# Two fused transformer blocks on one core: the last feature tile moved to the end of first products, and one-hot work moved from GpSimd to VectorE

## The chip, the core and the metric

The program runs on one core of a Trainium2 chip. A core has a matrix engine (TensorE, in rows PE; its weight loads are PEld), VectorE (DVE), ScalarE (ACT), GpSimd (POOL) and SyncE (SP, which here only issues DMAs). The engines work side by side; each takes its own instructions strictly in order and waits on semaphores for the others. The metric is the device time of one execution in microseconds (us).

## What is computed

A sequence of 512 tokens of width 1024 goes through two blocks. The first has a mixer (latent attention beside retention) and then a layer of 16384 small experts, of which each token uses 128: eight heads pick 16 experts each by two top-16 searches over 128 keys. The second block has pooling and sparse attention, and a feed-forward layer. The part that the change touches most is the expert layer:

```python
v1, i1 = lax.top_k(s1, PEER_TOPK)
v2, i2 = lax.top_k(s2, PEER_TOPK)
cand = (v1[..., :, None] + v2[..., None, :]).reshape(T, PEER_HEADS, PEER_TOPK * PEER_TOPK)
sc, ci = lax.top_k(cand, PEER_TOPK)
e1 = jnp.take_along_axis(i1, ci // PEER_TOPK, axis=-1)
e2 = jnp.take_along_axis(i2, ci % PEER_TOPK, axis=-1)
eidx = (e1 * PEER_NKEYS + e2).reshape(T, PEER_HEADS * PEER_TOPK)
gates = jax.nn.softmax(sc, axis=-1)
...
act = jax.nn.gelu(jnp.einsum('td,tkd->tk', xt, peer_u[it]), approximate=False)
return jnp.einsum('tk,tkd->td', gt * act, peer_v[it])
```

## The kernel before

Products in float32 accuracy are made from two rounded parts of each operand, a high and a low one (`wh` and `wl` for weights, and likewise for activations). `fm` (line 245) makes one product of 128 output features as three passes over the 8 tiles of the inner dimension: high by high, high weights by low activations, low weights by high activations, 24 matmuls in all. `split` (lines 210 and 211) makes the parts: ScalarE rounds the high part, and VectorE or GpSimd subtracts it for the low part (`wl`).

`residual` (line 367) is the product that ends a layer and is added to the stream: eight products over the activation tiles that the step ahead of it has just made. It is called six times: after the mixer of block one (activations `mgh`/`mgl`), after that of block two (`m2h`/`m2l`), and once for each of the four quarters of the feed-forward layer (`fh`/`fl`). In its first product, k = 0, the last of the eight tiles is the one made last.

In the expert layer, three token tiles (t = 0, 1, 2) are multiplied with all experts in turn, and the fourth (t = 3) gathers the rows of its experts. The stage between the queries and the big loop over experts does four things at once:

- `topkeys` and `topk` (VectorE): the searches, and then for each tile the picks, lines 1043 to 1055: a one-hot `oh` of 128x1024 by comparison (VectorE, line 1048), its product with the key numbers (GpSimd, line 1052, in four pieces of 128x256), and a sum over the one-hot (VectorE, line 1054). There are four such picks per tile and 16 in all.
- `spread` (line 1069): for 16 tokens at a time, four steps of one one-hot tile (`oh12` in the code, `oh` in rows) on VectorE (line 1077), four scalings of 128x128 with the gates (ScalarE, line 1083; for the third tile, t = 2, two of the four on GpSimd, line 1080), four small matmuls (line 1086, eight records in the trace for the four) and a copy to `stg` (ScalarE, line 1087); after four steps a DMA stores `stg` to `gates` in DRAM. A tile has 32 steps and the three tiles have 96.
- `front` (line 937): for one of the first 64 expert groups, a 512 KB load of `u_T`, its split (`wh` on ScalarE, `wl` on GpSimd), a product of 24 matmuls into `pu`, and a Gelu on ScalarE. Fronts 31 to 63 store their activations to DRAM (`ahead`).
- `step` (line 1106) decides in which program order these are interleaved: a front is added whenever `len(done_u) * PACE < steps + LEAD`. There are some 220 steps (19 of `topk` and 16 of `topkeys` per tile, 32 of `spread`), so that with `PACE` 3.6 the 64 fronts are all issued by the last step.

Outside the big loop the framework's scheduler then orders each engine's instructions; SyncE's DMAs stand in one queue as well. After the stage, the loop (`gated_acts`, `products`, rows `py`) loads `v` rows (`vr`) and the stored gates (`gin`), multiplies the activations with the gates on VectorE (line 1148), rounds them on ScalarE (`ah`) and multiplies.

Of the kernel before, what the change touches and what calls it, by code (L numbers as in the profile page):

```python
# [14 lines left out]
OP = mybir.AluOpType  # L15
AX = mybir.AxisListType

P = 128
T = 512
# [4 lines left out]
KD = D // P  # L24
# [142 lines left out]
def build(tc, A, OUT):  # L167
    nc = tc.nc
    es = ExitStack()
    V, S, G, TE = nc.vector, nc.scalar, nc.gpsimd, nc.tensor  # L170
# [71 lines left out]
        TE.matmul(out, lh, rl, start=False, stop=False)  # L242
        TE.matmul(out, ll, rh, start=False, stop=last)

    def fm(out, w, act, c0, t0, n, kt=KD, hooks=()):

        for i, (a, b) in enumerate(((0, 0), (0, 1), (1, 0))):
            for k in range(kt):
                TE.matmul(out, w[a][k][:, c0:c0 + P], act[b][k][:, t0:t0 + n],  # L249
                          start=i == 0 and k == 0, stop=i == 2 and k == kt - 1)  # L250
            if i < len(hooks):
                hooks[i]()

    def tm(out, w, act, c0, n, t0, m, kt=KD):

# [111 lines left out]
    def residual(get, act, sqs=None, norm=None):  # L367


        def done(k):  # L370
            def f(ps, a, b):
                V.tensor_tensor(h1[k][:, a:b], ps[:, a:b], h1[k][:, a:b], op=OP.add)  # L372
                if sqs:
                    sqs.add(h1[k], V if k > KD - 3 else G, a, b, k == KD - 1)
            return f
        for k in range(KD - 2 if sqs else KD):
            w, c0 = get(k)
            ps = mmps()
            fm(ps, w, act, c0, 0, T)
            done(k)(ps, 0, T)  # L380
        if sqs:
            js = [(mmps(), *get(k), done(k)) for k in (KD - 2, KD - 1)]
            for i, (a, b) in enumerate(HALVES):
                for j, (ps, w, c0, f) in enumerate(js):
                    fm(ps[:, a:b], w, act, c0, a, b - a, hooks=(lambda: norm.row(0),) if i and j else ())
                    f(ps, a, b)
                    if i and not j:
                        norm.cols(0)
# [116 lines left out]
    c = ks(half_slot("ckv", F32R))  # L505
# [7 lines left out]
    for a, b in PIECES:  # L513
        ps = mmps()
# [6 lines left out]
    for t0, t1, m in ((0, NT, P), (NT, NT + 1, M)):  # L521
        h = t1 - t0
# [86 lines left out]
    for h in range(8):  # L609
        b = 64 - h % 2 * 64  # L610
# [122 lines left out]
    for h in range(8):  # L733
# [11 lines left out]
        b = h % 2 * 64  # L745
# [65 lines left out]
    for h in range(8):  # L811
        w = wfm("w_rg", h)
        ps = mmps()
# [183 lines left out]
    def topk(t):  # L997

        val, idx = tops[t]


        cand = tn.tile([P, 8, 80], F32, name="cand", bufs=1)
        for o, a, na, nb_ in ((0, 0, 1, 16), (16, 1, 7, 8), (72, 8, 8, 1)):
            dst = cand[:, :, o:o + na * nb_].rearrange("p h (a b) -> p h a b", a=na)
            V.tensor_tensor(dst, val[:, 0, :, a:a + na, None].to_broadcast([P, 8, na, nb_]),
                            val[:, 1, :, None, :nb_].to_broadcast([P, 8, na, nb_]), op=OP.add)
        yield
        sel = tn.tile([P, 8, 16], F32, name="sel", bufs=1)
        pos = tn.tile([P, 8, 16], U32, name="pos", bufs=1)
        for h in range(8):  # L1010
            sc_ = tn.tile([P, P], F32, name="tscr", tag="tscr", bufs=2)
            top16(sel[:, h], pos[:, h], cand[:, h], sc_[:, :80])
            yield

        gate = tn.tile([P, 8, 16], F32, name="gate", bufs=1)
        V.tensor_tensor(gate, sel, sel[:, :, 0:1].to_broadcast([P, 8, 16]), op=OP.subtract)
        S.activation(gate, gate, AF.Exp)
        gs = tn.tile([P, 8], F32, name="gs", bufs=1)
        V.tensor_reduce(gs, gate, axis=AX.X, op=OP.add)
        V.reciprocal(gs, gs)  # L1020
        V.tensor_tensor(gate, gate, gs[:, :, None].to_broadcast([P, 8, 16]), op=OP.mult)
        yield

        pu = pos.rearrange("p h j -> p (h j)")
        row = tn.tile([P, 128], U32, name="prow", tag="tscr", bufs=2)
        col = tn.tile([P, 128], U32, name="pcol", tag="tscr", bufs=2)
        V.tensor_single_scalar(row, pu, 3, op=OP.logical_shift_right)
        V.tensor_single_scalar(col, pu, 7, op=OP.bitwise_and)
        af = tn.tile([P, 128], F32, name="af", bufs=1)
        bf = tn.tile([P, 128], F32, name="bf", bufs=1)  # L1030
        x = tn.tile([P, 128], F32, name="rk1", bufs=1)
        V.scalar_tensor_tensor(x, row, 9.0, col, op0=OP.is_equal, op1=OP.mult)
        V.tensor_scalar(af, row, 1.0, 0.0, op0=OP.subtract, op1=OP.max)
        V.tensor_tensor(af, af, x, op=OP.add)
        V.tensor_scalar(bf, row, 1.0, 8.0, op0=OP.is_equal, op1=OP.mult)
        V.tensor_tensor(x, col, x, op=OP.subtract)
        V.tensor_tensor(bf, bf, x, op=OP.add)
        yield

        idf = tn.tile([P, 2, 128], F32, name="idf", bufs=1)  # L1040
        V.tensor_copy(idf, idx.rearrange("p b h j -> p b (h j)"))
        ef = tn.tile([P, 2, 128], F32, name="ef", bufs=1)
        for b, rk_ in ((0, af), (1, bf)):
            iv = idf[:, b].rearrange("p (h r) -> p h r", h=8)
            for c in range(2):
                r_ = rk_[:, 64 * c:64 * c + 64, None]
                oh = tn.tile([P, 64, 16], F32, name="oh", bufs=2)
                V.tensor_tensor(oh, iota[:, None, :16].to_broadcast([P, 64, 16]), r_.to_broadcast([P, 64, 16]),
                                op=OP.is_equal)
                ov = oh.rearrange("p (h j) r -> p h j r", h=4)  # L1050
                for h in range(4):
                    G.tensor_tensor(ov[:, h], ov[:, h], iv[:, 4 * c + h, None].to_broadcast([P, 16, 16]), op=OP.mult)  # L1052
                yield
                V.tensor_reduce(ef[:, b, 64 * c:64 * c + 64], oh, axis=AX.X, op=OP.add)
                yield
        if t == GT:
            V.scalar_tensor_tensor(ef[:, 0], ef[:, 0], float(P), ef[:, 1], op0=OP.mult, op1=OP.add)
            V.tensor_copy(eg, ef[:, 0])
            V.tensor_copy(gg, gate.rearrange("p h j -> p (h j)"))
            return  # L1060
        pt = tpps()
        TE.transpose(pt[:, 0:P], ef[:, 0], ident)
        TE.transpose(pt[:, P:2 * P], ef[:, 1], ident)
        TE.transpose(pt[:, 2 * P:3 * P], gate.rearrange("p h j -> p (h j)"), ident)
        eT = tn.tile([P, 3, P], F32, name="eT", bufs=2)
        V.tensor_copy(eT, pt[:, :3 * P].rearrange("p (a t) -> p a t", a=3))
        picks[t] = eT

    def spread(t):
        NPL = (0, 0, 2)[t]  # L1070

        t0, eT = t * P, picks[t]
        for b0 in range(0, P, TB):
            stg = tn.tile([P, P, TB], F32, name="stg", bufs=2)
            for q0 in range(0, TB, 4):
                a1 = tn.tile([P, 2, 4, P], F32, name="oh12", bufs=4)
                V.tensor_tensor(a1, iota[:, None, None, :].to_broadcast([P, 2, 4, P]),  # L1077
                                eT[:, :2, b0 + q0:b0 + q0 + 4, None].to_broadcast([P, 2, 4, P]), op=OP.is_equal)
                for q in range(NPL):
                    G.tensor_tensor(a1[:, 1, q], a1[:, 1, q], eT[:, 2, b0 + q0 + q:b0 + q0 + q + 1].to_broadcast([P, P]),  # L1080
                                    op=OP.mult)
                for q in range(NPL, 4):
                    S.activation(a1[:, 1, q], a1[:, 1, q], AF.Copy, scale=eT[:, 2, b0 + q0 + q:b0 + q0 + q + 1])
                ps = mmps()
                for q in range(4):
                    TE.matmul(ps[:, q * P:(q + 1) * P], a1[:, 1, q], a1[:, 0, q], start=True, stop=True)  # L1086
                S.copy(stg[:, :, q0:q0 + 4], ps.rearrange("p (q e) -> p e q", q=4))
                yield
            nc.sync.dma_start(gd[:, :, (t0 + b0) // TB].rearrange("g p x -> p g x"),
                              stg.rearrange("p (g e) t -> p g (e t)", e=NE))  # L1090
# [8 lines left out]
        for x in g:  # L1099
            yield from x  # L1100

    PACE, LEAD = 3.6, 10
    steps = [0]

    def step():
# [60 lines left out]
    with tc.manual_schedule(engines={mybir.EngineType.Pool, mybir.EngineType.DVE}):  # L1166
        parts, u = gated_acts(0), u_of(AHEAD)
        for e in range(P - 2):
# [10 lines left out]
            while len(todo) > max(0, min(ngather, (P - 3 - e) * ngather // (P - 2 - G0))):  # L1179
                src, f, k = todo.pop(0)  # L1180
# [96 lines left out]
    kt = pool("keytmp", stack=stk)  # L1277
# [22 lines left out]
    for x in range(2):  # L1300
# [8 lines left out]
        for hf in range(2):  # L1309
            w = sp_.tile([P, 8, 256], F32, name="wc1", tag="h")  # L1310
            nc.sync.dma_start(w.rearrange("p l c -> p (l c)"), A["w_c1"][x][:, hf * 2048:(hf + 1) * 2048])
            w1.append(w)
    for br in range(2):
        w = wfm("w_kv", 2 * br)
        ps = mmps()
# [3 lines left out]
        for g in range(2):  # L1319
            a, b = slice(g * 64, g * 64 + 64), slice(64 - g * 64, 128 - g * 64)  # L1320
# [4 lines left out]
        w = wfm("w_kv", 2 * br + 1)  # L1325
        ps = mmps()
# [10 lines left out]
    w = wfm("w_gn", 0, width=48)  # L1337
    ps = mmps()
# [11 lines left out]
    ps = bank("s", "hid")  # L1350
# [149 lines left out]
    for g in range(4):  # L1500
        w = wfm("w_u", g)
        ps = mmps()
# [21 lines left out]
    for g, d in enumerate(pooled):  # L1524
        ps = bank("s", "yp")
# [43 lines left out]
    for b in range(4):  # L1569
        f = tuple(ks(slot(n, F32R)) for n in ("fh", "fl"))  # L1570
        for c in range(4):
# [4 lines left out]
            else:  # L1576
                for j in range(2):
                    ps = mmps()
# [47 lines left out]
```

## Time and profile before

| | |
|---|---|
| median of 3 runs | 2754.16 us (2748.56 to 2754.52) |
| the profiled execution | 2753.92 us |
| its span, first to last instruction | 2752.1 us |
| TensorE busy / its weight loads | 95% / 81% of the span |
| VectorE, ScalarE, GpSimd busy | 61%, 42%, 37% |
| mean granted TensorE clock | 0.977 of full speed |

The time of the profiled execution holds 1.8 us beside its span. The busy share of TensorE says little by itself, since its matmuls overlap and their ends are modelled; where it stood still is read from the chain of waits and from the idle times.

### The profile page before, as it was taken

The page shows a single profiled execution, that of the slowest core. Times are in us where ns is not written, and L with a number is a line of the kernel's source. Part 1 is how long each engine was busy: PE and PEld are TensorE (multiplying, and loading weights), DVE is VectorE, ACT ScalarE, POOL GpSimd, SP SyncE. Part 2 cuts the span into 40 slices and gives each one's busy share as a digit, 9 for nine tenths or more (in the row PEclk, how much of TensorE's full clock was granted, in tenths as well). Part 3 has the DMA queues.
Part 4 walks back from the last instruction along what each step waited for, and adds up shares of the span by engine and source line. Part 5 has one row for each costly group of instructions (what it writes and reads, how often), then busy time and mean ns, then how long its engine had stood idle before and what let it go on. Part 6 is the DMA issues. An engine that isn't in the chain of part 4 may idle for free.

```text
span 2752.1 us, 37185 instructions
## 1 busy us (share of the span) xinstructions
PE 2611.7 (95%) x13809; PEld 2239.1 (81%) x13809; DVE 1685.1 (61%) x3302; ACT 1149.3 (42%) x2096; POOL 1018.1 (37%) x735
## 2 busy tenths in 40 slices
PE   7899999999898998999999999998999999999998
PEld 6668778798898887888888888887666787878886
DVE  5672442248797863788888888886678422533433
ACT  4462332243676553333333333333677422423322
POOL 3322132326546690355555554552222233211111
PEclk9999999999999999999999999998999999999999
DMA  3312123323355567799999998983211123222221
GB/s 110 106 58 82 65 73 126 113 83 101 113 168 174 173 188 269 254 364 387 362 361 334 337 335 321 332 313 116 58 32 36 50 93 98 108 92 92 92 97 57
DMA packets 175653, 462.65 MB, mean 168 GB/s; under 512 B 15600, under 2 KB 76656, under 8 KB 168816
## 3 DMA queue, kind: packets, MB, share of 16 engines
q1 hardware_dynamic: 135152, 321.30, 33.4%
q0 software_dynamic: 36864, 134.23, 13.9%
q10 hardware_dynamic: 3456, 4.76, 0.7%
q8 instruction: 108, 1.77, 0.3%
q14 instruction: 73, 0.60, 0.1%
HBM read 419.59 MB, written 35.85 MB: 165 GB/s over the span
## 4 chain that ended last, share of the span: by engine, by line
PE 68%; DVE 10%; POOL 6%; issue 5%; DMA 4%; ACT 3%; ACTq 0%; SPq 0%; DVEq 0%; POOLq 0%
PE mm L249 34%; PE pu L249 12%; PE py L1158 11%; PE mm L1086 2%; POOL oh L1052 2%; POOL row L957 2%; PE o L1484 1%; PE tp L1479 1%; DVE row L962 1%; POOL wl L211 1%; DMA act<-ahead 1%; DVE vl L211 1%; DMA t<-t 1%; DVE oh L1077 1%; POOL oh L1080 1%
## 5 line engine op out<-in xcount | busy, mean ns | idle before, releaser
L211 POOL TENSOR_TENSOR wl<-wr,wh 128x1024 fp32r<-128x1024 f32 (+3 forms) x135 | 324.2, 2402 | 551.0 <-ACT wh L210 241.6
L210 ACT CAST wh<-wr 128x1024 fp32r<-128x1024 f32 (+2 forms) x271 | 274.3, 1012 | 411.4 <-PE mm L249 209.0
L249 PE MATMUL pu<-xf,wh 128*128 128x384 f32 x2048 | 392.4, 344 | 6.8 <-ACT act L944 6.8
L249 PEld LDWEIGHTS pu<-xf,wh 128*128 128x128 f32 x2048 | 362.9, 191 | 13.1 <-ACT act L944 7.9
L957 POOL DMA_INDIRECT row<-in_u_rows_dram,eg x128 | 187.2, 1463 | 245.5 <-DVE row L962 218.8
L957 POOL DMA_INDIRECT row<-in_v_rows_dram,eg x128 | 194.8, 1522 | 187.2 <-DVE yg L972 160.3
L211 DVE TENSOR_TENSOR wl<-wr,wh 128x1024 fp32r<-128x1024 f32 (+2 forms) x136 | 161.0, 1184 | 103.8 <-PE mm L249 63.6
L249 PE MATMUL pu<-xf,wl 128*128 128x384 f32 x1024 | 206.9, 345 | 14.7 <-POOL wl L211 14.0
L1158 PE MATMUL py<-vh,ah 128*128 128x512 f32 x768 | 198.8, 394 | 21.1 <-ACT ah L210 20.2
L249 PEld LDWEIGHTS pu<-xf,wl 128*128 128x128 f32 x1024 | 185.8, 193 | 18.2 <-POOL wl L211 17.0
L1158 PE MATMUL py<-vl,ah 128*128 128x512 f32 x768 | 198.0, 392 | 1.0 <-DVE vl L211 1.0
L1158 PE MATMUL py<-vh,al 128*128 128x512 f32 x768 | 196.0, 390 | 0.0
L210 ACT CAST vh<-vr 128x1024 fp32r<-128x1024 f32 x128 | 134.6, 1052 | 139.5 <-PE py L1158 74.2
L211 DVE TENSOR_TENSOR vl<-vr,vh 128x1024 fp32r<-128x1024 f32 x128 | 156.2, 1220 | 57.0 <-ACT vh L210 56.9
L1158 PEld LDWEIGHTS py<-vh,ah 128*128 128x128 f32 x768 | 143.3, 189 | 50.5 <-ACT ah L210 24.5
L1077 DVE TENSOR_TENSOR oh<-iota,eT 128x1024 f32<-128x1024 f32 x96 | 159.3, 1687 | 40.0 <-PE mm L1086 23.6
L210 ACT CAST ah<-act 128x384 fp32r<-128x384 f32 x128 | 65.6, 513 | 266.9 <-DVE act L1148 258.7
L1158 PEld LDWEIGHTS py<-vl,ah 128*128 128x128 f32 x768 | 145.5, 190 | 32.0 <-DVE vl L211 1.4
L1158 PEld LDWEIGHTS py<-vh,al 128*128 128x128 f32 x768 | 144.6, 188 | 30.1
L972 DVE SCALAR_TENSOR_TENSOR yg<-row,ag,yg 128x1024 f32<-128x1024 f32 x127 | 164.9, 1298 | 5.2 <-DMA row<-in_v_rows_dram,eg 2.9
L962 DVE SCALAR_TENSOR_TENSOR row<-row,xg 128x1024 f32<-128x1024 f32 x128 | 151.4, 1219 | 7.3 <-DMA row<-in_u_rows_dram,eg 7.2
L372 DVE TENSOR_TENSOR h<-mm,h 128x512 f32<-128x512 f32 (+1 forms) x54 | 34.1, 632 | 184.7 <-PE mm L249 184.7
(458 smaller groups left out, 5172.2 us busy)
## 6 DMA issues: line engine op xcount, KB each, us to landing
wr<-in_u_T_dram SPq DMA_DIRECT2D x128, 512.0 KB, 4.6
vr<-in_v_rows_dram SPq DMA_DIRECT2D x128, 512.0 KB, 6.3
wwr<-in_w_f_dram SPq DMA_DIRECT2D x32, 1024.0 KB, 4.8
gates<-stg SPq DMA_DIRECT2D x24, 1024.0 KB, 7.1
gin<-gates SPq DMA_DIRECT2D x16, 1536.0 KB, 10.6
wr<-in_w_gm_dram SPq DMA_DIRECT2D x16, 512.0 KB, 3.4
ahead<-act SPq DMA_DIRECT2D x33, 192.0 KB, 2.9
act<-ahead SPq DMA_DIRECT2D x33, 192.0 KB, 7.7
```

What stands on the lines that cost most here:

```text
L210: S.copy(hi, src)
L211: (lo_eng or V).tensor_tensor(lo, src, hi.bitcast(F32), op=OP.subtract)
L249: TE.matmul(out, w[a][k][:, c0:c0 + P], act[b][k][:, t0:t0 + n], start=i == 0 and k == 0, stop=i == 2 and k == kt - 1)
L372: V.tensor_tensor(h1[k][:, a:b], ps[:, a:b], h1[k][:, a:b], op=OP.add)
L957: G.indirect_dma_start(out=r, out_offset=None, in_=src, in_offset=bass.IndirectOffsetOnAxis(ap=eg[:, k:k + 1], axis=0))
L962: V.scalar_tensor_tensor(r, r, 1.0, xg, op0=OP.mult, op1=OP.mult, accum_out=ag[:, k:k + 1])
L972: V.scalar_tensor_tensor(yg[0], r, ag[:, k:k + 1], yg[0], op0=OP.mult, op1=OP.add)
L1052: G.tensor_tensor(ov[:, h], ov[:, h], iv[:, 4 * c + h, None].to_broadcast([P, 16, 16]), op=OP.mult)
L1077: V.tensor_tensor(a1, iota[:, None, None, :].to_broadcast([P, 2, 4, P]), eT[:, :2, b0 + q0:b0 + q0 + 4, None].to_broadcast([P, 2, 4, P]), ...
L1080: G.tensor_tensor(a1[:, 1, q], a1[:, 1, q], eT[:, 2, b0 + q0 + q:b0 + q0 + q + 1].to_broadcast([P, P]), op=OP.mult)
L1086: TE.matmul(ps[:, q * P:(q + 1) * P], a1[:, 1, q], a1[:, 0, q], start=True, stop=True)
L1158: TE.matmul(py[2 * t + d], x[:, t * P:(t + 1) * P], w[:, d * 512:(d + 1) * 512], start=e == 0 and i == 0, stop=e == P - 1 and i == 2)
```

## The change

The product of one-hot and key numbers in the picks goes from four GpSimd instructions to one on VectorE. The two scalings per step that GpSimd did for the third tile go to VectorE as `tensor_scalar`. `PACE` rises from 3.6 to 4.0, so that some 58 of the 64 fronts are issued by the last step and six follow it. And the first product of each `residual` handles the last activation tile after all passes over the other seven, with the pass over low weights ahead of that over low activations.

```diff
-    def fm(out, w, act, c0, t0, n, kt=KD, hooks=()):
-
-        for i, (a, b) in enumerate(((0, 0), (0, 1), (1, 0))):
-            for k in range(kt):
-                TE.matmul(out, w[a][k][:, c0:c0 + P], act[b][k][:, t0:t0 + n],
-                          start=i == 0 and k == 0, stop=i == 2 and k == kt - 1)
-            if i < len(hooks):
-                hooks[i]()
+    def fm(out, w, act, c0, t0, n, kt=KD, hooks=(), late=0):
+
+
+        for tiles in (range(kt - late), range(kt - late, kt)):
+            for i, (a, b) in enumerate(((0, 0), (1, 0), (0, 1)) if late else ((0, 0), (0, 1), (1, 0))):
+                for k in tiles:
+                    TE.matmul(out, w[a][k][:, c0:c0 + P], act[b][k][:, t0:t0 + n],
+                              start=i == 0 and k == 0, stop=i == 2 and k == kt - 1)
+                if i < len(hooks) and not late:
+                    hooks[i]()
+            if not late:
+                break
...
-            fm(ps, w, act, c0, 0, T)
+            fm(ps, w, act, c0, 0, T, late=1 if k == 0 else 0)
...
-                for h in range(4):
-                    G.tensor_tensor(ov[:, h], ov[:, h], iv[:, 4 * c + h, None].to_broadcast([P, 16, 16]), op=OP.mult)
+                V.tensor_tensor(ov, ov, iv[:, 4 * c:4 * c + 4, None].to_broadcast([P, 4, 16, 16]), op=OP.mult)
...
-                for q in range(NPL):
-                    G.tensor_tensor(a1[:, 1, q], a1[:, 1, q], eT[:, 2, b0 + q0 + q:b0 + q0 + q + 1].to_broadcast([P, P]),
-                                    op=OP.mult)
-                for q in range(NPL, 4):
+                for q in range(NV):
+                    V.tensor_scalar(a1[:, 1, q], a1[:, 1, q], eT[:, 2, b0 + q0 + q:b0 + q0 + q + 1], None, op0=OP.mult)
+                for q in range(NV, 4):
...
-    PACE, LEAD = 3.6, 10
+    PACE, LEAD = 4.0, 10
```

GpSimd's queue from the start of the stage, before, where `wl` is a front's low weights and `oh<-oh,idf` are the pieces of a pick:

```order
L211 TENSOR_TENSOR wl<-wr,wh 128x1024 x13
L1052 TENSOR_TENSOR oh<-oh,idf 128x256 x8
L211 TENSOR_TENSOR wl<-wr,wh 128x1024
L1052 TENSOR_TENSOR oh<-oh,idf 128x256 x8
L211 TENSOR_TENSOR wl<-wr,wh 128x1024 x7
L1052 TENSOR_TENSOR oh<-oh,idf 128x256 x3
```

and of the change, up to the first row gathers of the loop:

```order
L211 TENSOR_TENSOR wl<-wr,wh 128x1024 x64
L961 DMA row<-in_u_rows_dram,eg 128x1024 x2
L211 TENSOR_TENSOR wl<-wr,wh 128x1024
L961 DMA row<-in_u_rows_dram,eg 128x1024 x2
L211 TENSOR_TENSOR wl<-wr,wh 128x1024
```

Nothing stands between the low weights any more, and the first gathers move ahead of the last three of them. The end of the stage on TensorE, before (`mm<-oh` are the last steps of `spread`, `pu` fronts, `py` the loop's first product):

```order
L1086 MATMUL mm<-oh_9609 128x128 x4
L1086 MATMUL mm<-oh_9621 128x128 x4
L1086 MATMUL mm<-oh_9633 128x128 x4
L249 MATMUL pu<-xf,wh 128x384 x32
L1158 MATMUL py_9658<-vh,ah 128x512
```

and of the change:

```order
L1088 MATMUL mm<-oh_9381 128x128 x4
L251 MATMUL pu<-xf,wh 128x384 x16
L251 MATMUL pu<-xf,wl 128x384 x8
...
L251 MATMUL pu<-xf,wh 128x384 x16
L251 MATMUL pu<-xf,wl 128x384 x8
L1160 MATMUL py_9610<-vh,ah 128x512
```

Before, two thirds of two more fronts (16 of their 24 matmuls each, of the loop's own) stood between the last step and the loop; now six whole fronts stand there, and the loop's own follow later. SyncE's queue at the same place, of the change (`gates` is the last store of the stage, `gin` the first load of the loop):

```order
L1091 DMA gates<-stg 128x16x128
L950 DMA ahead<-act 128x384
L222 DMA wr<-in_u_T_dram 128x1024
L222 DMA vr<-in_v_rows_dram 128x1024
L1147 DMA gin<-gates 128x3072
L950 DMA ahead<-act 128x384 x2
```

The load of the gates stands ahead of the stores of the last five fronts, where it stood behind the last of all before. The first product of the first feed-forward quarter on TensorE, before (`fh`, `fl` are the activations, `wwh`, `wwl` the weights):

```order
L249 MATMUL mm<-fh,wwh 128x512 x10
L249 MATMUL mm<-fl,wwh 128x512 x8
L249 MATMUL mm<-fh,wwl 128x512 x8
L249 MATMUL mm<-fh,wwh 128x512 x6
```

and of the change:

```order
L251 MATMUL mm<-fh,wwh 128x512 x7
L251 MATMUL mm<-fh,wwl 128x512 x7
L251 MATMUL mm<-fl,wwh 128x512 x7
L251 MATMUL mm<-fh,wwh 128x512
L251 MATMUL mm<-fh,wwl 128x512
L251 MATMUL mm<-fl,wwh 128x512
```

Before, the scheduler had already put two matmuls of the second product in front; now 21 matmuls of the first product stand ahead of the one that needs the last tile.

## Rows read from the trace of the kernel before

**Rows 1.** The page, part 1: busy us, share of the span, instructions.

```profile
PE 2611.7 (95%) x13809; PEld 2239.1 (81%) x13809; DVE 1685.1 (61%) x3302; ACT 1149.3 (42%) x2096; POOL 1018.1 (37%) x735
```

**Rows 2.** Busy time by stretch of the stage: us, busy (instructions), granted clock, DMA.

```profile
618.80:690.50 71.70, 64.35 (x345) 62.84 (x343) 58.33 (x275) 23.90 (x30) 45.60 (x30) 0.95 0.30 100
690.50:815.00 124.50, 118.31 (x735) 116.09 (x736) 103.27 (x295) 86.74 (x212) 64.37 (x34) 0.96 0.47 142
815.00:938.00 123.00, 115.99 (x727) 113.96 (x726) 98.53 (x280) 83.61 (x196) 67.04 (x39) 0.97 0.58 175
938.00:1039.70 101.70, 90.20 (x566) 87.14 (x565) 64.98 (x52) 55.56 (x121) 87.96 (x89) 0.95 0.59 176
```

**Rows 3.** Groups by form in the stage, 618.8 to 1039.7 us.

```profile
L211 POOL TENSOR_TENSOR wl<-wr,wh 128x1024 fp32r<-128x1024 f32 x63 | 161.8, 2569 | 122.8 <-ACT wh L210 80.3 <-PE pu L249 35.5 <-ACT oh L1083 3.5
L1052 POOL TENSOR_TENSOR oh<-oh,idf 128x256 f32<-128x256 f32 x64 | 60.3, 974 | 22.2 <-DVE oh L1048 22.2
L1080 POOL TENSOR_TENSOR oh<-oh,eT 128x128 f32<-128x128 f32 x64 | 45.0, 733 | 5.7 <-DVE oh L1077 5.7
...
L1077 DVE TENSOR_TENSOR oh<-iota,eT 128x1024 f32<-128x1024 f32 x96 | 159.3, 1687 | 40.0 <-PE mm L1086 23.6 <-ACT stg L1087 5.0 <-POOL oh L1080 4.7
L1054 DVE TENSOR_REDUCE ef<-oh 128x64 f32<-128x1024 f32 x16 | 19.5, 1219 | 32.8 <-POOL oh L1052 32.7
...
L249 PE MATMUL pu<-xf,wl 128*128 128x384 f32 x512 | 106.7, 352 | 14.0 <-POOL wl L211 14.0
L1086 PE MATMUL mm<-oh 128*128 128x128 f32 x768 | 102.0, 282 | 11.2 <-POOL oh L1080 6.0 <-ACT oh L1083 5.0
L988 PE MATMUL mm<-keyst,pq 128*128 128x256 f32 x37 | 10.0, 391 | 0.0
```

**Rows 4.** Timeline of VectorE and GpSimd in the first picks: start, duration, instruction.

```profile
650.11 2.40 POOL L211 TENSOR_TENSOR wl<-wr,wh 128x1024 fp32r<-128x1024 f32 x1 [2.68 <-PE pu L249]
650.22 2.44 DVE L1016 TENSOR_TENSOR gate<-sel 128x128 f32<-128x128 f32 x1
...
657.24 0.28 DVE L1021 TENSOR_TENSOR gate<-gate,gs 128x128 f32<-128x128 f32 x1
657.91 1.22 DVE L1048 TENSOR_TENSOR oh<-iota,af 128x1024 f32<-128x1024 f32 x1
```

**Rows 5.** A VectorE scaling of 128x128 elsewhere in the kernel, by form.

```profile
L1467 DVE TENSOR_SCALAR s<-s,sm 128x128 f32<-128x128 f32 x24 | 5.6, 295 | 0.1
```

**Rows 6.** The chain of waits through the end of the stage: start, duration, what.

```profile
991.73 0.89 PE mm L1086 x8
992.62 4.20 PE pu L249 x24
...
1039.70 7.02 DMA gates<-stg
1046.79 9.19 DMA gin<-gates
1057.24 10.10 PE py L1158 x36
...
1068.74 8.20 PE py L1158 x36
```

**Rows 7.** Timeline of TensorE at the first products of the first four residuals.

```profile
513.32 0.50 PE L249 MATMUL mm<-mgh,wh 128*128 128x512 f32 x1 [2.15 <-ACT mgh L840]
2322.58 0.50 PE L249 MATMUL mm<-m2h,wh 128*128 128x512 f32 x1 [1.68 <-ACT m2h L840]
2426.58 0.79 PE L249 MATMUL mm<-fh,wwh 128*128 128x512 f32 x1 [3.99 <-ACT fh L210]
2513.62 4.46 PE L249 MATMUL mm<-fh,wwh 128*128 128x512 f32 x18
```

**Rows 8.** Busy time and granted clock just behind two of those waits.

```profile
513.30:518.20 4.90, 4.88 (x14) 3.88 (x15) 0.69 (x1) 1.05 (x1) 0.00 (x0) 0.65 0.16 67
2426.60:2429.60 3.00, 3.00 (x7) 2.42 (x8) 0.65 (x1) 0.00 (x0) 0.00 (x0) 0.51 0.83 333
```

More of the change, by code (lines that the diff above doesn't have):

```diff
@@ L1069, in spread @@
     def spread(t):
-        NPL = (0, 0, 2)[t]
+        NV = (0, 0, 2)[t]
         t0, eT = t * P, picks[t]
```

## The prediction

> **What bounds the kernel now.** I read the page first: TensorE is busy 95% of the span, the others far less [rows 1]. A gain must therefore come from places where TensorE stands still or runs at half its clock, so I looked next for its idle times and their releasers. The change touches two kinds of places.
>
> The first is the stage of picks and spreads. By the chain it runs from the first front at 618.8 us to the loop's first product at 1057.24, which is 438.4 us. I cut it where a token tile's spread begins, into four stretches [rows 2]: the first has no spread, the next three have one each. Their lengths are 71.7, 124.5, 123.0 and 101.7 us. The work that TensorE must do there is smaller. A front takes 4.20 us when nothing holds it, a step of spread 0.89 [rows 6]: 64 x 4.20 + 96 x 0.89 = 354, and the key products are some 13 us (37 take 10.0 [rows 3], another 12 of them the rest, taken at the same price), together 367. At the end it also does 32 matmuls of the loop's own fronts, 5.6 us by the same price. So 438.4 - 367 - 5.6 = 66 us are waiting or half clock. The rows name the causes: 14.0 us until GpSimd has made the low weights `wl`, 6.0 until it has scaled a one-hot, and 5.0 for one-hots that ScalarE scales [rows 3]. The granted clock of 0.95 to 0.97 [rows 2] costs about 4% of 421 us, 17 us. The largest single wait stands at the end: the last store of the gates takes 7.02 us, their load 9.19, and the loop's first product waits for both [rows 6].
>
> GpSimd is the engine that is late. It spends 60.3 us on pieces of picks and 45.0 on scalings, between low weights of 2.57 us each, and VectorE waits 32.7 us for the picks [rows 3]. In the last stretch it is busy 88.0 of 101.7 us, more than VectorE's 65.0 [rows 2].
>
> The second kind is the first product of a residual. Four of six wait for the last tile: 2.15, 1.68 and 3.99 us, and the last quarter of the feed-forward layer repeats the 3.99. The two quarters between them don't wait, since the scheduler put 18 matmuls of two products in front [rows 7].
>
> **The change, part by part.** *VectorE in the stage.* By the four stretches it is busy 58.3 + 103.3 + 98.5 + 65.0 = 325 us. Part of this is waiting beside GpSimd: a 128x128 operation that takes 0.28 us alone took 2.44 beside a `wl` of 2.40, and a one-hot that takes 1.22 alone [rows 4] has a mean of 1.69 over the 96 of the spreads [rows 3], which is 45 us lost there; counting the small operations of the picks at the same rates I estimate 62 in all. GpSimd is busy 267 us by its three rows [rows 3], so 0.23 us are lost for each of its microseconds. After the change only the low weights are left there, 58 x 2.4 = 139 us in the stepped part: 32 us lost, and I take 40, because the moved work is of the kind that loses. The moved work is 16 products of 128x1024. No row has this one; the nearest is the comparison of the same shape with two broadcast operands, 1.22 us [rows 4], hence 20 us. It also includes 64 scalings of 128x128, for which the nearest row gives 5.6 / 24 = 0.23 us in line and 0.295 each [rows 5]: 15 to 19, and I take 17. The bound from below is no loss beside GpSimd at all, the one from above 2.4 us for each of the 80. VectorE's new sum is 325 - 62 + 40 + 20 + 17 = 340 us, of which 62, 105, 100 and 72 by stretch (the cut in lost time falls mostly in the last, where the 45 us of scalings stood).
>
> *TensorE in the stage.* With 4.0 in place of 3.6 steps per front, the first stretch has 11.4 fronts: 48 us, and 5 of keys, 53. The next two have 16.75 each: 70.4 + 28.5 + 4 = 103. The last has 12.75: 53.6 + 28.5 = 82. The sum is 341 for 58 fronts.
>
> A stretch can't be shorter than the longer of the two engines, and I add what I think is left of the waits between them: 62 + 4 (of keys, which queue behind fronts) = 66, 105 + 6 = 111, 103 + 6 = 109, and 82 + 13 = 95 for the last, whose first half holds picks, spread and the moved scalings together, so that VectorE sets it there. That is 381 us to the last step, against 420.9.
>
> *The tail.* Six fronts follow the last step: 25.2 us, and 1.3 for a wait between them. Beside them the last gates are stored and loaded: from the store's start at 1039.70 to the first product it was 17.5 us, 7.02 and 9.19 of DMA and 1.3 for the multiplication and rounding [rows 6]; with the copy ahead of it I estimate 18.5. The load now stands in SyncE's queue ahead of five stores that wait for fronts, so 18.5 is hidden in 26.5; if that cover were gone, the loop would begin some 18 us later. ScalarE's queue has the loop's first rounding ahead of the last three Gelus, which therefore end about a microsecond late; two `pu` banks cover that.
>
> So the loop's first product begins 381 + 26.5 = 407.5 us after 618.8, which is 30.9 earlier. The 5.6 us done ahead for the loop must be done later, and the first 36 products of the loop take 10.10 us where the next 36 take 8.20 [rows 6], so 1.9 of half clock comes back. The stage gives 30.9 - 5.6 + 1.9 = 27 us.
>
> *The residuals.* 18 matmuls take 4.46 us [rows 7], and from their start to the next group's it is 4.3, so 0.24 each at most; I take 0.23. 21 of them, 4.8 us, now stand before the one that needs the last tile, where 9 or 10 stood. At the first two this hides the wait, 2.15 and 1.68. Behind the first the clock was 0.65 over 4.9 us [rows 8], 1.7 lost, which doesn't come up any more. At the third and sixth the 12 more are 2.8 us of the 3.99, so 1.2 of the wait remains; with 1.5 of half clock behind it (0.51 over 3.0 us [rows 8]) that is 4.3, twice: 8.6. At the fourth and fifth nothing is saved. The low weights, needed earlier than before, are made a product ahead: no loss. The sum is 2.15 + 1.7 + 1.7 + 8.6 = 14 us.
>
> Together 41 us: 2753.9 - 41 = **2713 us**. The profiled execution is within 0.3 us of the median shown, so this holds for both. A change of 0.2%, 5.5 us, is what a measurement of this kernel can tell from none.
>
> *A rule that speaks against it.* The rows show that VectorE waits for a whole GpSimd instruction [rows 4]. The Trainium skill, in SBUF — State Buffer, section Who interferes with whom, says why: a VectorE instruction with two inputs in SBUF, or a `tensor_scalar` in its two-port mode, shares a port with GpSimd, and the one that comes first holds it to its end. All 80 moved operations are of these kinds, while the sums that they join are not. The trace agrees for the comparisons; no run here shows it for `tensor_scalar` beside `wl`.
>
> **The rivals.**
>
> *TensorE sets every stretch.* If VectorE's loss falls with GpSimd's load and the queues run ahead of each other, the stretches are 62, 105, 103 and 84, 354: 2713 - 27 = 2686 us. For it: 20 of TensorE's idle microseconds are GpSimd's by name [rows 3], and some of the half clock goes with them. Against it: VectorE's sum, 340, is as long as TensorE's. Chance 0.17.
>
> *VectorE takes over from GpSimd.* With 340 us it is as long as TensorE, each waits for the other in turn, and as much as now is lost in the stepped part, 54 us: 341 + 54 = 395, 14 more, 2727; up to 2745 if the last stretch is VectorE's alone. For it: VectorE had 96 us idle before, and has 41 left by my sum. Chance 0.25.
>
> *Slower: the moved work queues behind the low weights.* If each of the 80 waited 1.2 us, half a `wl`, beyond what I counted, VectorE would have 436 us; the stepped part would be 441 with the little waits, and the time 2713 + 60 = 2773. It decides from some 0.6 us per operation, where the 41 us and the 5.5 are gone. Against it: the one-hots lost 0.47 each beside twice the GpSimd load. Chance 0.06.
>
> *The residuals gain nothing,* because a new wait for low weights or the last low tile takes the old one's place: 2727. Chance 0.07.
>
> *The tail isn't covered,* because the load of the gates or the rounding is held by something in a queue: 18 us lost, 2731. Chance 0.05.
>
> **How the numbers follow.** My forecast has 0.40. The range of 2686 to 2745 holds it and all rivals but the slower one and the edges of two others. Faster by over 0.2%: all but the slower case and a small part of the second rival, 0.88; within 0.2%: 0.05; slower: 0.07.
>
> **What would show it.** GpSimd has no work but `wl` until the loop; TensorE's 14.0 us until `wl` shrinks below 3, and its wait ahead of the loop, now 17.5 less the 5.6 of early fronts, is gone; the stage from first front to first `py` is near 408 us; the mean of the comparisons falls from 1.69 towards 1.5; the first residual product waits for nothing in four of six cases and some 1.2 us in two. The prediction is wrong if VectorE's busy time in the stage is far over 340, if stretches of the stage keep their length though GpSimd is free, or if the loop itself gets longer.

## The result, and the profile after

The changed kernel takes 2722.66 us, median of 4 runs (2718.19 to 2726.24), against 2754.34 us for the kernel before (4 runs beside them): a ratio of 0.9885, with a 95% interval of 0.9859 to 0.9911. It is 31.7 us faster; the forecast was 41. The profiled execution took 2725.69 us, and its span is 2723.9, which is 28.2 less than before. The four runs span 8 us, with a mean granted clock of 0.981 in the two longer and of 0.983 and 0.984 in the two shorter; the profiled one, from which the rows below are read, is among the longer.

The page of the changed kernel, part 1 (busy us, share of the span, instructions), answers to [rows 1].

```profile
PE 2602.1 (96%) x13809; PEld 2234.7 (82%) x13809; DVE 1720.7 (63%) x3382; ACT 1150.2 (42%) x2096; POOL 928.7 (34%) x607
```

GpSimd has 128 instructions and 89 us less, VectorE 80 instructions and only 36 us more. Nothing here says where the 31.7 us come from. That is read from the stretches, which answer to [rows 2] and have the same columns (length, busy PE, PEld, DVE, ACT and POOL, granted clock, DMA share, GB/s). They are cut where a spread's first product is evicted, within 3 us of the cuts of before, and the fifth is the tail up to the loop's first product.

```profile
615.80:685.10 69.30, 59.42 (x331) 58.40 (x330) 69.12 (x288) 23.69 (x33) 31.36 (x13) 0.93 0.30 98
685.10:795.20 110.10, 105.16 (x667) 102.56 (x666) 106.24 (x285) 81.09 (x199) 44.44 (x16) 0.98 0.49 148
795.20:908.20 113.00, 107.72 (x696) 106.49 (x695) 98.35 (x256) 81.04 (x197) 52.97 (x17) 0.98 0.60 182
908.20:1002.70 94.50, 83.71 (x534) 82.40 (x533) 87.97 (x155) 55.54 (x119) 36.69 (x13) 0.95 0.58 168
1002.70:1036.00 33.30, 28.06 (x145) 27.40 (x145) 6.27 (x7) 11.09 (x15) 16.23 (x10) 0.90 1.00 361
```

The four stretches are 386.9 us long, 34 less than the 420.9 of before, of which the six fronts that now stand behind them are 25. VectorE has taken GpSimd's place: it is busy 69.1 of 69.3 us in the first stretch and 88.0 of 94.5 in the last. The stage is 420.2 us, where it was 438.4.

The groups by form in the four stretches answer to [rows 3].

```profile
L211 POOL TENSOR_TENSOR wl<-wr,wh 128x1024 fp32r<-128x1024 f32 x59 | 168.2, 2852 | 221.9 <-ACT wh L210 144.1 <-PE pu L251 55.8 <-PE mm L1088 15.3
L1080 DVE TENSOR_TENSOR oh<-iota,eT 128x1024 f32<-128x1024 f32 x96 | 146.5, 1543 | 18.6 <-PE mm L1088 18.5
...
L251 PE MATMUL pu<-xf,wl 128*128 128x384 f32 x464 | 92.9, 342 | 4.7 <-POOL wl L211 4.7
...
L1083 DVE TENSOR_SCALAR oh<-oh,eT 128x128 f32<-128x128 f32 x64 | 33.4, 566 | 0.1
L1055 DVE TENSOR_TENSOR oh<-oh,idf 128x1024 f32<-128x1024 f32 x16 | 24.6, 1543 | 0.0
L1057 DVE TENSOR_REDUCE ef<-oh 128x64 f32<-128x1024 f32 x16 | 19.2, 1207 | 0.0
L1066 PE MATMUL tp<-cstt,ef 128*128 128x128 f32 x3 | 1.2, 390 | 8.2 <-DVE ef L1057 8.2
```

VectorE's sums of picks (L1057) wait for nothing where they waited 32.8 us, and TensorE's wait for low weights falls from 14.0 us to 4.7. New is 8.2 us on the transposition of picks (L1066): TensorE now waits for VectorE. The 64 moved scalings (L1083) take 0.566 us each.

A timeline of VectorE and GpSimd in the last spread (start, duration, instruction) shows why.

```profile
962.74 0.49 DVE L1083 TENSOR_SCALAR oh<-oh,eT 128x128 f32<-128x128 f32 x2
...
964.45 3.25 POOL L211 TENSOR_TENSOR wl<-wr,wh 128x1024 fp32r<-128x1024 f32 x1 [3.43 <-ACT wh L210]
...
965.41 5.12 DVE L1083 TENSOR_SCALAR oh<-oh,eT 128x128 f32<-128x128 f32 x4
...
967.89 2.35 POOL L211 TENSOR_TENSOR wl<-wr,wh 128x1024 fp32r<-128x1024 f32 x1 [0.20 <-ACT wh L210]
```

Two scalings take 0.49 us where GpSimd is idle, and four take 5.12 us beside two low weights. Counted in the trace, 53 of the 64 run clear of a `wl` and have a mean of 0.27 us; the other 11 overlap one and have 1.97. Ten of these end 0.08 to 0.09 us after the `wl` that they stand beside: a scaling that starts beside a low weight takes as long as the low weight still runs.

The chain of waits through the tail answers to [rows 6].

```profile
1002.67 4.22 PE pu L251 x24
...
1009.87 7.34 DMA vr<-in_v_rows_dram
...
1017.24 0.04 ACT vh L210
...
1019.23 0.40 ACT act L948
...
1019.65 0.32 SPq L950
...
1020.07 7.97 DMA wr<-in_u_T_dram
...
1029.21 6.74 PE pu L251 x24
1035.95 8.19 PE py L1160 x36
```

The store and load of the gates are gone from the chain, and the loop's first 36 products take 8.19 us where they took 10.10. In their place the last front is late. It waits for its weights, whose load was issued at 1020.07 behind a store (line 950), which waited for a Gelu, which stood behind the loop's first rounding `vh`, which waited for its own load. The front then takes 6.74 us in place of 4.22, at a granted clock of 0.63. The timelines of ScalarE and TensorE show the two waits:

```profile
1017.24 1.05 ACT L210 CAST vh<-vr 128x1024 fp32r<-128x1024 f32 x1 [5.57 <-DMA vr<-in_v_rows_dram]
...
1029.21 5.33 PE L251 MATMUL pu<-xf,wh 128*128 128x384 f32 x16 [5.07 <-ACT wh L210]
```

TensorE at the first products of the first three residuals, against [rows 7].

```profile
514.66 0.39 PE L251 MATMUL mm<-mgh,wh 128*128 128x512 f32 x1
...
2305.98 0.39 PE L251 MATMUL mm<-m2h,wh 128*128 128x512 f32 x1
...
2407.05 0.50 PE L251 MATMUL mm<-fh,wwh 128*128 128x512 f32 x1 [1.34 <-ACT fh L210]
```

Each row is the first matmul that needs the last tile. The waits of 2.15 and 1.68 us are gone, and 1.34 is left of 3.99 (at the sixth residual it is 1.39). The granted clock behind the first and the third, against [rows 8], is 1.00 where it was 0.65 and 0.51:

```profile
513.70:518.60 4.90, 4.90 (x22) 3.73 (x21) 2.61 (x3) 2.21 (x3) 0.05 (x1) 1.00 0.46 159
2407.00:2410.00 3.00, 2.96 (x12) 2.15 (x13) 1.39 (x2) 0.00 (x0) 0.00 (x0) 1.00 0.87 333
```

### The profile page after: what moved, and what is told of

Same layout as the page of the kernel before. It is cut to its first block, busy times and chain, and to the rows that moved or that the text cites. A ratio compares the mean times of both kernels' runs of the same rounds, so it can differ in the third digit from the quotient of the medians.

```text
span 2723.9 us, 37103 instructions
## 1 busy us (share of the span) xinstructions
PE 2602.1 (96%) x13809; PEld 2234.7 (82%) x13809; DVE 1720.7 (63%) x3382; ACT 1150.2 (42%) x2096; POOL 928.7 (34%) x607
## 4 chain that ended last, share of the span: by engine, by line
PE 69%; DVE 12%; issue 6%; DMA 3%; POOL 3%; ACT 3%; ACTq 0%; SPq 0%; DVEq 0%; POOLq 0%
PE mm L251 34%; PE pu L251 12%; PE py L1160 11%; PE mm L1088 2%; POOL row L961 2%; PE o L1486 2%; PE tp L1481 1%; DVE row L966 1%; DVE oh L1080 1%; DMA act<-ahead 1%; DVE vl L211 1%; DVE oh L1083 1%; POOL wl L211 1%; DMA t<-t 1%; DMA wr<-in_u_T_dram 1%
## 5 line engine op out<-in xcount | busy, mean ns | idle before, releaser
L211 POOL TENSOR_TENSOR wl<-wr,wh 128x1024 fp32r<-128x1024 f32 (+3 forms) x135 | 340.5, 2523 | 657.4 <-ACT wh L210 321.0
L1080 DVE TENSOR_TENSOR oh<-iota,eT 128x1024 f32<-128x1024 f32 x96 | 146.5, 1543 | 18.6 <-PE mm L1088 18.5
```

What stands on the lines that cost most here:

```text
L211: (lo_eng or V).tensor_tensor(lo, src, hi.bitcast(F32), op=OP.subtract)
```

## The experiments

All times are medians, and all ratios are to the kernel before on the same chip. Their intervals are some 0.1 to 0.25% to either side, so 3 to 7 us. The changed kernel's own is 7 us to either side. By an estimate from these intervals a variant of it has to differ from it by some 9 us before its time tells the two apart. Only the last experiment does; for the others the medians and the rows of single executions are signs, not proof.

**The four edits, each alone on the kernel before.** The late tiles alone (with `fm` as in the change):

```diff
-            fm(ps, w, act, c0, 0, T)
+            fm(ps, w, act, c0, 0, T, late=1 if k == 0 else 0)
```

> The kernel before with the late last tiles alone. My theory: the four waits of the residuals (2.15, 1.68, 3.99, 3.99 us) shrink as they do in the changed kernel and half of the saving is half clock, so the time falls by 14 us (11 to 16). Rival: the wait is only passed to the next product or the norm behind it, and the time is within 4 us of before.

Measured: 2742.43 us, ratio 0.9957 [0.9944, 0.9970], so 11.8 us (8 to 15). The timeline of this kernel has the same remaining wait as the changed one:

```profile
2420.49 0.50 PE L251 MATMUL mm<-fh,wwh 128*128 128x512 f32 x1 [1.34 <-ACT fh L210]
```

The rival, that the wait is passed on, falls.

The pick products alone:

```diff
-                for h in range(4):
-                    G.tensor_tensor(ov[:, h], ov[:, h], iv[:, 4 * c + h, None].to_broadcast([P, 16, 16]), op=OP.mult)
+                V.tensor_tensor(ov, ov, iv[:, 4 * c:4 * c + 4, None].to_broadcast([P, 4, 16, 16]), op=OP.mult)
```

> The kernel before with the pick products alone on VectorE. My theory: the 32.8 us that VectorE waits for GpSimd's picks go, 25 us of products come (16 x 1.54), and the stage from the first front to the loop's first product gets 5 to 15 us shorter; the wait ahead of the loop stays. Rival: VectorE was the bound of the first stretches all the same and only swaps its waiting for work: within 4 us of before.

Measured: 2741.21 us, ratio 0.9953 [0.9941, 0.9966], 13.0 us, at the upper end of what was expected; the stage is 423.7 us, some 15 less than before. In its groups the sums of picks no longer wait:

```profile
L1053 DVE TENSOR_REDUCE ef<-oh 128x64 f32<-128x1024 f32 x16 | 19.3, 1209 | 0.1
```

The scalings alone:

```diff
-                for q in range(NPL):
-                    G.tensor_tensor(a1[:, 1, q], a1[:, 1, q], eT[:, 2, b0 + q0 + q:b0 + q0 + q + 1].to_broadcast([P, P]),
-                                    op=OP.mult)
-                for q in range(NPL, 4):
+                for q in range(NV):
+                    V.tensor_scalar(a1[:, 1, q], a1[:, 1, q], eT[:, 2, b0 + q0 + q:b0 + q0 + q + 1], None, op0=OP.mult)
+                for q in range(NV, 4):
```

> The kernel before with the 64 scalings of the last spread alone moved from GpSimd to VectorE. My theory: GpSimd, busy 88 of 101.7 us in the last stretch, loses 45 us there, VectorE gets some 33 (64 x 0.52), and the last stretch is 3 to 8 us shorter. Rival: each scaling waits for a low weight or a pick on GpSimd, VectorE becomes the bound of the last stretch, and the time is the same or up to 8 us longer.

Measured: 2748.54 us, ratio 0.9981 [0.9973, 0.9990], 5.2 us, as the theory has it (3 to 8).

The pace alone:

```diff
-    PACE, LEAD = 3.6, 10
+    PACE, LEAD = 4.0, 10
```

> The kernel before with 4.0 in place of 3.6 steps per front alone. My theory: six fronts stand behind the last step and cover the gates' store and load, so the 12.6 us of waiting ahead of the loop fall to about 5, 1.9 us of half clock go with it, and the 5.6 us of the loop's early fronts come back: 3 to 8 us shorter. Rival: the steps are bound by VectorE and GpSimd, which keep their length with fewer fronts between them, so the fronts that are moved behind them only add there: 5 to 12 us longer.

Measured: 2751.22 us, ratio 0.9983 [0.9973, 0.9992], 4.7 us, within the theory's 3 to 8. Its chain already has the late last front of the changed kernel, so that wait comes with the pace and not with the moved work:

```profile
1031.71 9.66 DMA wr<-in_u_T_dram
...
1042.55 6.78 PE pu L249 x24
```

Each edit gains alone. The four sum to 34.7 us; the change has 31.7, and the intervals don't tell these two apart.

**Two edits taken back from the changed kernel.** The pace:

```diff
-    PACE, LEAD = 4.0, 10
+    PACE, LEAD = 3.6, 10
```

> The changed kernel with 3.6 steps per front as before (late tiles, picks and scalings moved). Theory of added gains: the pace is worth here what it was worth alone, 4.7 us, so the time is 2727 to 2728. Rival, that the tail of the changed kernel has a wait of its own (5.1 us ahead of the last front, and a front at half clock) and VectorE sets the stretches: the pace gains nothing here, 2719 to 2724.

Measured: 2723.71 us, ratio 0.9887 [0.9871, 0.9904]. The scalings back on GpSimd (the diff of the scalings above, reversed):

> The changed kernel with two of four scalings of the last spread on GpSimd as before. Theory of added gains: the time rises by the 5.2 us that the scalings' move was worth alone, to 2728. Rival: with the picks gone GpSimd has room (36.7 of 94.7 us busy in the last stretch) and VectorE has not (88.2 of 94.7), so the move was worth nothing behind the picks' move: within 3 us of 2723, and the mean one-hot of the spreads rises from 1.54 towards 1.69 us.

Measured: 2719.34 us, ratio 0.9874 [0.9858, 0.9891]. By the medians both rivals hold: behind the other edits neither shows what it was worth alone, and the scalings do no better on VectorE than on GpSimd. The times alone don't settle it, by the estimate above. The rows side with the rivals: the stage is 421.1 us with the old pace against 420.2, and the last stretch 92.0 us with GpSimd's scalings against 94.5. The one-hots are longer again, as that rival said:

```profile
L1080 DVE TENSOR_TENSOR oh<-iota,eT 128x1024 f32<-128x1024 f32 x96 | 159.2, 1683 | 23.9 <-PE mm L1089 16.7 <-POOL oh L1083 7.2
```

96 x 0.14 = 13 us longer there, against the 33.4 us of scalings that VectorE no longer does, while GpSimd needs 48 for them.

**The tail.** The stores of activations are moved to ScalarE's queue:

```diff
-            nc.sync.dma_start(ad[e - HOLD], a)
+            nc.scalar.dma_start(ad[e - HOLD], a)
```

> The changed kernel with the stores of the fronts' activations issued by ScalarE, right behind their Gelu, and not by SyncE. Theory: the last front's weights are late because their load stands in SyncE's queue behind two stores that wait for ScalarE; with the stores elsewhere the wait of 5.1 us ahead of that front and the 2.5 us of half clock in it go, so the tail falls from 33 to 26 us and the time by 5 to 8. Rival: the load is slow because the DMA engines are full (8 us for one tile of weights beside the gates and the row loads), and leaving its queue earlier it only lands as late: within 3 us of the changed kernel.

Measured: 2722.48 us, ratio 0.9892 [0.9875, 0.9908]: no gain in the median, as the rival had it. In the chain the load of the last front's weights is issued at 1009.39 in place of 1020.07, but takes 12.94 us in place of 7.97. So it lands 5.7 us sooner, not as late as before, and the tail of this execution is 29.9 us in place of 33.3; the theory's mechanism is there in part.

```profile
1009.39 12.94 DMA wr<-in_u_T_dram
```

ScalarE's timeline shows the second half of the stall:

```profile
1014.68 1.04 ACT L210 CAST vh<-vr 128x1024 fp32r<-128x1024 f32 x1 [8.11 <-DMA vr<-in_v_rows_dram]
1015.63 1.04 ACT L210 CAST wh<-wr 128x1024 fp32r<-128x1024 f32 x1
1016.58 0.48 ACT L948 ACTIVATE act<-pu 128x384 f32<-128x384 f32 x1
```

ScalarE stands 8.11 us at the loop's first rounding until `vr` has landed, with the next front's weights and a Gelu queued behind it. TensorE's timeline has the front that waits for that Gelu's bank:

```profile
1017.11 3.07 PE L251 MATMUL pu<-xf,wh 128*128 128x384 f32 x16 [3.19 <-ACT act L948]
```

A longer lead moves two fronts out of the tail:

```diff
-    PACE, LEAD = 4.0, 10
+    PACE, LEAD = 4.0, 16
```

> The changed kernel with a lead of 16 steps in place of 10, so that one or two more fronts stand in the first stretch and as many fewer in the tail. Theory: VectorE sets the first stretch (70.4 of 70.6 us busy) and TensorE idles 10 us in it, so the fronts fit there for nothing, and the tail is shorter by one or two fronts, less what the gates' path then shows: 2 to 5 us faster. Rival: the low weights of the added fronts hold VectorE up by as much, and the gates' path shows in the tail: same, or up to 4 us slower.

Measured: 2714.14 us, ratio 0.9866 [0.9849, 0.9884], 8.5 us below the changed kernel by the medians and 5 by the ratios, where the theory had 2 to 5. The first stretch and the tail:

```profile
616.00:691.30 75.30, 68.48 (x379) 67.75 (x378) 66.80 (x303) 26.87 (x37) 37.57 (x15) 0.95 0.30 104
...
998.20:1019.70 21.50, 20.31 (x116) 19.98 (x115) 2.34 (x3) 6.92 (x11) 13.45 (x9) 1.00 1.04 362
```

TensorE does 9.1 us more in the first stretch for 6.0 more of time, and the tail is 11.8 shorter, as its stall is gone too. The path of the gates then shows in the loop, on TensorE's timeline:

```profile
1028.36 2.08 PE L1160 MATMUL py<-vh,ah 128*128 128x512 f32 x4 [4.40 <-ACT ah L210]
```

**The price of the scalings.** All four on ScalarE, as in the spreads before:

```diff
-        NV = (0, 0, 2)[t]
+        NV = (0, 0, 0)[t]
```

> The changed kernel with all four scalings of the last spread on ScalarE, as in the two spreads before it, so no tensor_scalar beside the low weights. Theory: VectorE sets the last stretch (88.2 of 94.7 us busy, 33.4 us of them scalings that take 0.57 us each in place of the 0.26 of their fastest) and ScalarE has room (55.7 busy, 25 to come), so the stretch falls to TensorE's 86 to 88: 2714 to 2717. Rival: the scalings queue on ScalarE behind evictions, roundings and Gelus, TensorE waits for them there, and the time is within 3 us of the changed kernel, or longer.

Measured: 2716.70 us, ratio 0.9862 [0.9840, 0.9884], 6 us below the changed kernel and within the theory's 2714 to 2717. The last stretch is 86.0 us in place of 94.5, and VectorE has 69 of it in place of 88:

```profile
906.20:992.20 86.00, 80.46 (x538) 79.76 (x537) 69.08 (x91) 70.98 (x179) 41.36 (x13) 0.98 0.65 201
```

The same with a lead of 16, and a lead of 16 with GpSimd's scalings (the diffs are those above):

> The changed kernel with a lead of 16 steps and all four scalings of the last spread on ScalarE. If the gains of the two add up: 2706 to 2710. Rival: the lead alone has filled what the scalings held up: 2713 to 2716.

> The changed kernel with a lead of 16 steps, and two of four scalings of the last spread on GpSimd as before. If the two gains measured behind the changed kernel (8.5 us by the lead, 3.3 by the scalings) come from different places, the first stretch with the tail and the last stretch, they add up: 2710 to 2712. Rival: both only take away the same wait of the tail: 2714 or more.

Measured: 2715.81 us, ratio 0.9856 [0.9834, 0.9878], and 2718.11 us, ratio 0.9879 [0.9855, 0.9903]. By the medians neither adds up, and the rivals' numbers hold. The lead, ScalarE's scalings and both together are between 2714 and 2717 us, which their intervals don't tell apart. Of the kernels that compute everything, the lead alone has the lowest median and the lead with ScalarE's scalings the lowest ratio.

**The contention.** GpSimd only fills the fronts' low weights:

```diff
-        (lo_eng or V).tensor_tensor(lo, src, hi.bitcast(F32), op=OP.subtract)
+        if lo_eng == 'zero':
+            G.memset(lo.bitcast(F32), 0.0)
+        else:
+            (lo_eng or V).tensor_tensor(lo, src, hi.bitcast(F32), op=OP.subtract)
...
-        u = u or u_of(e, G)
+        u = u or u_of(e, 'zero')
```

> The changed kernel in which GpSimd fills the fronts' low weights with zeros and doesn't compute them, so that it reads no SBUF there (the low part of the fronts' weights is left out of the computation; all matmuls stay). Theory: the term that I mis-sized is VectorE's loss beside the low weights. Then the one-hots fall from 1.54 to 1.22 to 1.25 us, the scalings from 0.57 to about 0.26, VectorE's sum over the four stretches from 362 to about 300, and the stretches to TensorE's 62, 105, 103 and 84: 20 to 33 us faster than the changed kernel, 2690 to 2703. Rival: not the contention but the order in which VectorE takes picks, top-k and one-hots sets the stretches; the instructions get shorter, but the time stays within 8 us of the changed kernel.

Measured: 2679.64 us, ratio 0.9724 [0.9700, 0.9747], 43 us below the changed kernel, more than the 20 to 33 expected. Its groups in the four stretches, and the stretches:

```profile
L1083 DVE TENSOR_TENSOR oh<-iota,eT 128x1024 f32<-128x1024 f32 x96 | 115.5, 1221 | 36.3 <-PE mm L1091 36.3
L212 POOL MEMSET wl<- 128x1024 f32 x58 | 55.6, 959 | 286.7 <-PE pu L254 280.5 <-PE mm L1091 6.2
L1058 DVE TENSOR_TENSOR oh<-oh,idf 128x1024 f32<-128x1024 f32 x16 | 19.5, 1222 | 0.0
L1086 DVE TENSOR_SCALAR oh<-oh,eT 128x128 f32<-128x128 f32 x64 | 16.4, 320 | 0.1
```

```profile
618.60:676.70 58.10, 57.99 (x330) 57.04 (x329) 56.01 (x288) 23.97 (x32) 11.44 (x12) 1.00 0.34 118
676.70:775.20 98.50, 98.50 (x653) 97.94 (x653) 85.98 (x284) 81.53 (x199) 15.23 (x16) 1.00 0.51 161
775.20:879.00 103.80, 103.80 (x685) 103.39 (x684) 81.47 (x256) 81.54 (x198) 16.18 (x17) 1.00 0.65 195
879.00:960.50 81.50, 81.50 (x557) 81.50 (x557) 66.99 (x155) 56.13 (x120) 12.68 (x13) 1.00 0.69 211
```

One-hots and pick products fall to the 1.22 us that [rows 4] show for a one-hot alone, and the 64 scalings from 33.4 to 16.4 us. VectorE's sum falls from 361.7 us to 290.5, TensorE has no idle time from the second stretch on, and the granted clock is 1.00 throughout. The four stretches are 341.9 us, which is the prediction's sum of TensorE's work in them, 341 (by stretch they lie up to 5 us apart). The run doesn't separate the contention from the low weights being ready sooner (0.96 us in place of 2.85), but for those TensorE waited only 4.7 us in the changed kernel. Nor does it separate the missing waits from the zeros as the reason for the clock of 1.00; the changed kernel, though, holds 1.00 with true weights over the first 120 us of its loop (1035.9 to 1155.9), in which TensorE never stands idle.

## Why the prediction was right, and where it was off

The direction, the main cause and the range held; the time is 9.7 us above the forecast of 2713 and nearer to the rival of 2727. Step by step:

*The residuals* held. 14 us were forecast and 11.8 (8 to 15) measured alone; in the two profiled executions what lies outside the stage and the loop is 13.7 us shorter (3.0 ahead of them, 10.7 behind). Two waits are gone, 1.34 and 1.39 us are left where 1.2 was expected, and the half clock behind them did not come up again.

*The loop* held. Its first 36 products take 8.19 us, so the 1.9 of half clock is back, and the work no longer done ahead is there: from the loop's first product to the second residual it is 1265.2 us (1035.95 to 2301.11) where it was 1261.4 (1057.24 to 2318.65), 3.8 more, with 5.6 - 1.9 = 3.7 forecast. One execution of each gives this difference, so that it is so close is partly luck.

*The stage* is the term of the sum that was mis-sized: it is 18.2 us shorter, not 30.9, and about 14 net of the loop, not 27. There are two parts.

- The four stretches are 386.9 us, 5.9 over the 381 forecast (66, 111, 109 and 95; measured 69.3, 110.1, 113.0 and 94.5). The excess stands in the first, where VectorE is busy 69.1 us and 62 were forecast, and in the third, where TensorE is busy 107.7 and 103 were forecast, while VectorE's 98.4 are near the forecast 100. VectorE's sum is 361.7, not 340. The step that failed is its loss beside the low weights ("I take 40"). Against the last experiment it is 71: 31 on the one-hots, 17 on the scalings, 5 on the pick products and 18 on other operations of the searches and picks. That is 0.42 us for each of the 168 that GpSimd spends on the low weights, where 0.23 were taken. The scalings had their price, 17 us for 64, from a row of another stage [rows 5]; they take 33.4. The bounds had the right neighbour, 2.4 us beside a `wl`; the sum didn't use it. And where the prediction says that no run shows a `tensor_scalar` beside `wl`, the trace of before did hold one, the last of four of its line, where the others take some 0.21 us:

```profile
942.28 2.37 POOL L211 TENSOR_TENSOR wl<-wr,wh 128x1024 fp32r<-128x1024 f32 x1
...
942.32 2.41 DVE L1035 TENSOR_SCALAR bf<-prow 128x128 f32<-128x128 uint32 x1
```

Of the 64 scalings 58 stand in the last stretch, where VectorE is busy 88.0 us and not 72. The 13 us of slack that I added there took up the difference, so its length came out right for the wrong reason: luck.

- The tail is 33.3 us, not 26.5. The gates were covered, as forecast. What failed is "two `pu` banks cover that": I counted the loop's first rounding on ScalarE as a microsecond of work and not as a wait. ScalarE stood 5.57 us until its load landed, with the last fronts' roundings and Gelus behind it; the last front then waited 5.07 us and took 2.5 longer at its lower clock, where 1.3 was taken for a wait. With stores elsewhere the same stall is seen, so SyncE's queue alone is not its cause. That putting the rounding behind the last Gelu would remove it was not tried. The trace of before already had this wait, hidden there behind that for the gates:

```profile
1048.30 1.04 ACT L210 CAST vh<-vr 128x1024 fp32r<-128x1024 f32 x1 [8.63 <-DMA vr<-in_v_rows_dram]
```

Of the prediction's own signs, the mean of the comparisons fell towards 1.5 (1.54) and the first residual products wait as it says. TensorE's wait for `wl` shrank to 4.7 us and not below 3, the stage is 420 us and not near 408, and VectorE's 361.7 us are 6% over the 340.

*The rivals.* "VectorE takes over from GpSimd" (2727) names what happened in the first and last stretches: VectorE is busy 69.1 of 69.3 and 88.0 of 94.5 us. "TensorE sets every stretch" (2686) is not what the change does, but it is where the kernel goes once the contention is gone: 2680, by the last experiment. The slower case would have needed 0.6 us more per moved operation; the scalings and the pick products both took some 0.3 more than forecast.

*The rule that speaks against it* bears out in its mechanism. The Trainium skill, SBUF — State Buffer, section Who interferes with whom, says that a VectorE instruction with two SBUF inputs contends with a GpSimd instruction that reads SBUF, and not with one that only writes it, while a `tensor_scalar` in a two-port mode shares the whole pair. The trace agrees: 34 of the 96 one-hots of the last experiment overlap a fill, and none takes over 1.24 us; a scaling beside a fill of 0.95 us does wait, as this timeline of it shows.

```profile
888.44 0.95 POOL L212 MEMSET wl<- 128x1024 f32 x1 [5.03 <-PE pu L254]
...
888.48 0.99 DVE L1086 TENSOR_SCALAR oh<-oh,eT 128x128 f32<-128x128 f32 x1
```

*What stays open.* The late tiles and the picks, each alone, sum to 24.8 us. No run has just these two, so it isn't shown how the other 7 of the 31.7 us divide between pace, scalings and the width of the measurements.

## What to carry to other kernels

Work that moves from GpSimd to VectorE while GpSimd keeps other work is to be priced from a row with that work beside it, not from one of another stage; the 64 small scalings here took 33.4 us beside it and 16.4 without. A mean hides how: most ran at full speed, and the few that started beside a low weight waited it out. Where one in-order queue serves two phases, ask of the first instruction of the next phase what it waits for, not how long it takes: its wait is paid by all that stands behind it. Edits that remove waits of one stage overlap: each of four gained alone, and two of them showed no gain behind the others.

## What the runs showed that was not expected

VectorE's loss beside the low weights was worth more than I reckoned even with the result at hand: where it is gone, VectorE is busy 71 us less in the four stretches and the stage is 50 us shorter (370.0 against 420.2). TensorE's granted clock goes from 0.93 to 0.98 in the stretches to 1.00, all of it at the upper level of 2.4 GHz; its waits between VectorE's products are gone too. GpSimd loses as well: its subtraction for a low weight, 2.569 us on average before, takes 2.852 after the change, though GpSimd has less to do. And a load of 512 KB of weights, which lands in a median of 4.6 us over the kernel before, took 7.97 us in the tail of the changed kernel, where the DMA engines are full (share 1.00 at 361 GB/s), and 12.94 us there with the stores moved (1.03 at 375).
